# Spacing the final LayerNorm on VectorE and re-pacing the output products of a mixed RG-LRU and attention layer

## The chip, the cores and the metric

The kernel runs on one core of a Trainium2 chip. The metric is device time in microseconds (us) for one execution of the whole layer, and the median of several runs is what is compared. The engines are named as the profile names them: PE (TensorE, matrix products; PEld are its weight loads), DVE (VectorE), ACT (ScalarE), POOL (GpSimd) and SP (SyncE, which here issues nearly all DMAs).

## The reference

One layer on x of 2048 rows and 1024 columns, in float32:

```
h = layer_norm(x) * (1 + scale) + shift          # scale, shift, gate from c
xr, zr, q, k, v, za, fl = split(h @ w_in)
y_r = rms_norm(rg_lru(conv(xr))) * silu(zr)      # 512 columns, recurrent half
y_a = rms_norm(forgetting_attention(q, k, v, log_sigmoid(fl))) * silu(za)   # 8 heads of 64
y   = concat(y_r, y_a) @ w_out
res = alpha * x + gate * y
out = layer_norm(res) * ln_gain + ln_bias
```

The attention is causal, with a decay term added to each score, and a softmax over the keys.

## The kernel before, in words

Every float32 matrix is split into a float16 high and low part, and a product is three matmuls (high by high, high by low, low by high). The change lies in the last phase, from about 560 us on, where attention, the projections of q, the output products and the final LayerNorm are woven into one stream.

The queries are cut into 4 chunks of 512 rows (`ci` = 0 to 3), and the work of the attention is a list of 32 items, chunk by chunk and head by head. An item (ci, h) has `4*ci + 4` steps, one for each block of 128 keys. A step is `s_t`: two matmuls of 512 columns into a PSUM tile `pst` (L1335, L1337), the exponential on ACT into `pf` (L1343), a cast on ACT to float16 into `ph` (L1345), and the low part of `ph` on POOL (L1347) or, each fourth step, on DVE (L1349). Five steps later `av` multiplies that block with V into two `acc` tiles. `fin` copies the sums and divides them (L1365 to L1370).

Ahead of each item runs its `maxpass`: the scores once more, into PSUM tiles `pmx`, whose row maxima DVE takes with `tensor_reduce` into `mc` (L1315, 4*(ci+1) of them per item); from these come `Z`, a small transpose into `pzt`, and one row of `qb` (L1330), which the item's own score products then subtract. So a group of four `pzt` matmuls marks the end of each item's maxima, 32 groups in all. `pst`, `pmx` and `pzt` share five PSUM banks (tag A).

Everything else is a side job: a list `side` of Python generators, of which `pump` runs the first one from one `yield` to the next. In its order the list holds the projections of q for chunks 1 to 3 (`q_unit`, 24 matmuls into one PSUM bank, tag O, then an eviction by ACT and DVE), the preparation of the weights `w_out`, and last `out_gen`, the output products. `out_gen` goes through 16 tiles of 128 rows. A tile has two halves of 512 columns; a half is 24 matmuls (`out_mm`: 12 on `yr`, the recurrent part, 12 on `yT`, the attention part), with three yields inside, then one DVE instruction that scales the sum and adds the residual (`xres`, L1524) and a yield. So a tile is 8 yields and 48 matmuls. `prep_a` loads `zs` and the residual `xres` of the next tile, `prep_b` and `prep_c` make its `yT` (ACT, four transposes `pyt` on PE into bank O, DVE, ACT, POOL). The tiles of a chunk can start only after that chunk's last head (`out_open`).

After its second half, a tile's LayerNorm is queued as `ln_gen`: statistics, then four DVE instructions of 128 by 512 elements, two that subtract the mean and multiply by the gain (L1438), two that scale by the inverse deviation and add the bias (L1442), and the store of the tile (L1445, an SP queue entry that waits for them). `out_gen` takes one step of the oldest `ln_gen` at each of its own yields.

How often `pump` is called is set in the main loop: at each of the steps `credit` grows by `todo / togo`, and `pump` is called once for each whole unit. From item (0,0) on this is (12*QU+32)/64 with QU = 5, from item (1,4) on 102/256, to the end. What is left after the last step runs then in one go.

All of this only gives the order in which the program is written. A scheduler then orders the instructions of each engine by dependencies, priorities and its own estimates; the engines run their queues in that order.

Of the kernel before, what the change touches and what calls it, by code (L numbers as in the profile page):

```python
# [26 lines left out]
TT = S // P  # L27
# [11 lines left out]
def hybrid_mixer(  # L39
# [921 lines left out]
    def q_unit(p, ci):  # L961
        w, u = take(("q", p))
        if p not in q_sc:
            q_sc[p] = cst([P, 1], f"fq{p}")
            nc.vector.tensor_tensor(q_sc[p], u, k_sc[p], ALU.mult)
        ps = pj_bank() if ci == 0 else bank("O", "pq")
        for _ in proj_1(ps, w, ci):
            yield
        hl = t2([P, 2, CH], "qhl", F16)
        split_out(hl[:, 0], hl[:, 1], ps, q_sc[p])  # L970
        qk_store([(qd, 0, 1)], p, hl, slice(ci * CH, (ci + 1) * CH))
        yield

    w_out_v = w_out.rearrange("(k p) n -> k p n", p=P)
    wocol = cst([P, KT], "wocol")
# [310 lines left out]
    def maxpass(ci, h, res):  # L1286
        n = cnt[0]
        cnt[0] += 1
        qb, z = QB[n % 4], Z[n % 4]
        sl = slice(ci * CH, (ci + 1) * CH)  # L1290
        nk = (ci + 1) * CH
        if ci < 2:
            kk = r4([P, 2, 2 * CH], "kk", F16)
        else:
            kk = sb.tile([P, 2, S], F16, name="kk", tag="H", bufs=8)
        nc.sync.dma_start(kk[:, 0, 0:nk], kd[h, :, 0:nk])
        nc.sync.dma_start(kk[0:DH, 1, 0:nk], kd[h, 0:DH, 0:nk])
        nc.sync.dma_start(kk[DH:DH + 3, 1, 0:nk], kb[h, :, 0:nk])
        nc.sync.dma_start(qb[0:DH, :], qd[h, DH:P, sl])
        qs = sb.tile([P, CH], F16, name="qs", tag="qs", bufs=3)  # L1300
        nc.sync.dma_start(qs, qd[h, :, sl])
        nc.gpsimd.memset(qb[DH:DH + 1, :], 0.0)
        res.append((kk, qb, qs))
        yield
        mc = sm([P, 4, 4], "mc")
        for i in range(4):
            nk = (4 * ci + i + 1) * P
            for b in range(ci + 1):
                w = min(CH, nk - b * CH)
                ps = bank("A", "pmx")  # L1310
                end = b == ci
                mm(ps[:, 0:w], qb[:, i * P:(i + 1) * P], kk[0:67, 1, b * CH:b * CH + w], True, not end)
                if end:
                    mm(ps[:, w - P:w], identb, maskn, False, True)
                nc.vector.tensor_reduce(out=mc[:, i, b:b + 1], in_=ps[:, 0:w], axis=AX.X, op=ALU.max)  # L1315
                yield
        if ci > 0:
            m = sm([P, 4], "mrow")
            nc.vector.tensor_reduce(out=m, in_=mc[:, :, 0:ci + 1], axis=AX.X, op=ALU.max)
        else:  # L1320
            m = mc[:, :, 0]
        nc.vector.tensor_scalar(z[:, :, DH], m, -1.0 / RS, ndc[:, ci, h:h + 1], ALU.mult, ALU.add)
        yield True
        yield True
        with tc.issue_after(last["pe"]):
            ps = bank("A", "pzt")
            for i in range(4):
                mm(ps[0:DH + 1, i * P:(i + 1) * P], z[:, i, 0:DH + 1], ident16, i == 0, i == 3, True)
        yield
        nc.scalar.copy(qb[DH:DH + 1, :], ps[DH:DH + 1, :])  # L1330
# [96 lines left out]
    def ln_gen(tt, xt):  # L1427
        st = sm([P, 2, 6], "bst")
        nc.vector.bn_stats(st[:, 0, :], xt[:, 0:CH])
        yield  # L1430
        nc.vector.bn_stats(st[:, 1, :], xt[:, CH:D])
        mv = sm([P, 2], "mv")
        nc.vector.bn_aggr(mv, st)
        rs = ln_rs(mv)
        yield
        for n in range(2):
            ns = slice(n * CH, (n + 1) * CH)
            nc.vector.scalar_tensor_tensor(xt[:, ns], xt[:, ns], mv[:, 0:1], late["lng"][:, ns], ALU.subtract, ALU.mult)  # L1438
            yield
        for n in range(2):  # L1440
            ns = slice(n * CH, (n + 1) * CH)
            nc.vector.scalar_tensor_tensor(xt[:, ns], xt[:, ns], rs, late["lnb"][:, ns], ALU.mult, ALU.add)  # L1442
            if n == 0:
                yield
        nc.sync.dma_start(out[tt * P:(tt + 1) * P, :], xt)  # L1445
# [8 lines left out]
    def out_mm(pq, yr, yT, i, ns):  # L1454
        for k in range(KT):
            if k < 4:
                yy = yr[:, k, :, i * P:(i + 1) * P]
            else:
                yy = yT[:, :, (k - 4) * P:(k - 3) * P]
            mm(pq, yy[:, 0, :], wo[k][:, 0, ns], k == 0, False)  # L1460
            mm(pq, yy[:, 0, :], wo[k][:, 1, ns], False, False)
            mm(pq, yy[:, 1, :], wo[k][:, 0, ns], False, k == KT - 1)
            if k % 2 == 1 and k < KT - 1:
                yield k

    def out_last(tt, yr, yT, xt):
# [17 lines left out]
        for ns in hs:  # L1484
            nc.vector.scalar_tensor_tensor(xt[:, ns], xt[:, ns], rs, late["lnb"][:, ns], ALU.mult, ALU.add)
            nc.sync.dma_start(out[tt * P:(tt + 1) * P, ns], xt[:, ns])

    def out_gen():
        lns = []

        def step_ln():
            if lns and next(lns[0], 0) == 0:
                lns.pop(0)

        for tt in range(TT):
            ci, i = tt // 4, tt % 4
            while ci not in outs:
                starved[0] = True
                step_ln()
                yield  # L1500
            starved[0] = False
            if tt not in yTs:
                prep_b(tt)
                yield
                prep_c(tt)
                yield
            yr = outs[ci][0]
            yT, xt = yTs[tt]
            if tt == TT - 1:
                for _ in out_last(tt, yr, yT, xt):  # L1510
                    step_ln()
                    yield
                break
            for n in range(2):
                ns = slice(n * CH, (n + 1) * CH)
                pq = bank("C" if ci == NC - 1 else "O", "pout")
                for k in out_mm(pq, yr, yT, i, ns):
                    yield
                    if n == 0 and k == 1:
                        prep_a(tt + 1)  # L1520
                    elif n == 0 and k == 3:
                        prep_b(tt + 1)
                    step_ln()
                nc.vector.scalar_tensor_tensor(xt[:, ns], pq, kap, xt[:, ns], ALU.mult, ALU.add)  # L1524
                if n == 0:
                    g = ln_gen(tt, xt)
                    next(g)
                    yield
                    prep_c(tt + 1)
                else:  # L1530
                    next(g)
                    lns.append(g)
                    yield
        while lns:
            step_ln()

    items = [(ci, h) for ci in range(NC) for h in range(H)]
    LOOK = 5
    QU = 5
    Y = {}  # L1540
    res = []
    side = []
# [70 lines left out]
    for n, (ci, h) in enumerate(items):  # L1613
# [4 lines left out]
                todo, togo = 12 * QU + 32, 8 * 4 + 4 * 8  # L1618
        if (ci, h) == (1, 4):
            todo, togo = 3 * 34, 4 * 8 + 8 * 12 + 8 * 16  # L1620
        while done < cum[n]:
            next(mg)
            done += 1
# [51 lines left out]
```

## Time and profile before

| What | us |
|---|---|
| median of 3 runs | 1149.67 (1149.29 to 1150.42) |
| the profiled execution's own time | 1150.82 |
| its span in the trace | 1149.1 |
| PE busy over the span | 1091.7 |
| DVE, ACT, POOL busy | 787.0, 707.1, 627.7 |

The page gives the busy time of each engine and its share, then slices of the span, the groups of instructions and the chain of work that ended last. A group's time is by kernel line and by tile names, so `pout` are the output products, `pst` and `acc` the attention's, `pmx` those of the row maxima. The views by windows give the same for chosen stretches of the span; the `pzt` groups are used here to cut the span between items. The granted clock is the share of TensorE's full clock in the stretch.

### The profile page before, as it was taken

To read this page: it belongs to the slowest core of one execution; us is meant where nothing else is said; L and a number is where in the kernel's file an instruction comes from. 1 tells how busy PE (TensorE), PEld (TensorE's weight loads), DVE (VectorE), ACT (ScalarE), POOL (GpSimd) and SP (SyncE) were. 2 spreads that over 40 slices of the span, in tenths; PEclk is the share of its full clock that TensorE was granted. 3 is DMA by queue.
4 is the path that set the end of the run, shared out by engine and by line. 5 is a ranking of instruction groups with operands and counts; after the bars stand their busy time and mean duration, and the time that the engine had idled before them with its cause. 6 is when DMAs were issued, how large, how long until landed. Compare 5 with 4: busy or idle time off the path is not lost.

```text
span 1149.1 us, 20239 instructions
## 1 busy us (share of the span) xinstructions
PE 1091.7 (95%) x7473; PEld 611.2 (53%) x7473; DVE 787.0 (68%) x1441; ACT 707.1 (62%) x1234; POOL 627.7 (55%) x655
## 2 busy tenths in 40 slices
PE   8989999999999999999989999999999989999897
PEld 5875544454544444444455545556555555655544
DVE  6878577776777973585287556777777777787546
ACT  3447737664767511543286668787778877787930
POOL 5725633454455300730279756777777676766731
PEclk8999999999999999999979999999999999999999
DMA  9853047220224711764154354333233142321011
GB/s 285 242 172 110 1 127 217 77 68 19 55 56 119 229 66 52 251 203 142 36 187 145 108 161 136 97 96 100 91 106 114 35 137 82 103 74 47 19 47 55
DMA packets 109415, 128.36 MB, mean 112 GB/s; under 512 B 10316, under 2 KB 79540, under 8 KB 109316
## 3 DMA queue, kind: packets, MB, share of 16 engines
q1 hardware_dynamic: 109088, 127.01, 36.2%
q8 instruction: 58, 0.95, 0.3%
q14 instruction: 41, 0.34, 0.1%
q10 hardware_dynamic: 228, 0.06, 0.0%
HBM read 97.57 MB, written 29.46 MB: 111 GB/s over the span
## 4 chain that ended last, share of the span: by engine, by line
PE 65%; DVE 11%; ACT 8%; issue 6%; POOL 5%; DMA 4%; SPq 0%; DVEq 0%; ACTq 0%; POOLq 0%
PE pj L93 25%; PE pout L93 12%; PE pst L93 8%; PE pq L93 6%; PE acc L93 5%; PE pmx L93 4%; DVE mc L1315 2%; POOL ph L1347 1%; PE pgate L93 1%; ACT pf L1343 1%; DVE xres L1442 1%; DMA zs<-zd 1%; POOL XL L636 1%; ACT ph L1345 1%; DVE wadab L648 1%
## 5 line engine op out<-in xcount | busy, mean ns | idle before, releaser
L93 PE MATMUL pj<-hT,wT 128*128 128x512 f16 x1440 | 321.1, 381 | 2.6 <-DVE sza L1192 2.6
L1347 POOL TENSOR_TENSOR ph<-pf,ph 128x512 f16<-128x512 f32 (+2 forms) x240 | 263.8, 1111 | 108.5 <-ACT ph L1345 92.6
L93 PEld LDWEIGHTS <-wT 128*128 128x128 f16 x1792 | 169.8, 98 | 205.3 <-issue 18.8
L1315 DVE TENSOR_REDUCE mc<-pmx 128x1 f32<-128x512 f32 (+2 forms) x320 | 183.3, 601 | 90.2 <-PE pmx L93 84.1
L1343 ACT ACTIVATE pf<-pst,bias 128x512 f32<-128x512 f32 (+1 forms) x320 | 194.3, 632 | 59.4 <-PE pst L93 57.7
L1345 ACT CAST ph<-pf 128x512 f16<-128x512 f32 (+1 forms) x320 | 173.3, 568 | 21.4 <-PE acc L93 15.4
L93 PE MATMUL acc<-V,ph 128*128 128x129 f16 (+1 forms) x2176 | 159.6, 209 | 9.0 <-POOL ph L1347 4.4
L93 PEld LDWEIGHTS <-ph 128*128 128x128 f16 x2176 | 126.5, 99 | 67.8 <-POOL ph L1347 8.8
L93 PE MATMUL pst<-qs,kk 128*128 128x512 f16 (+1 forms) x320 | 111.6, 351 | 4.1 <-DVE mc L1315 2.9
L93 PE MATMUL pst<-qb,kk 65*128 65x512 f16 (+1 forms) x320 | 110.5, 354 | 0.9 <-ACT qb L1330 0.8
L93 PE MATMUL pmx<-kk,qb 67*128 67x512 f16 (+2 forms) x320 | 104.1, 353 | 4.5 <-DVE mc L1315 2.7
L93 PE MATMUL pout<-wo,yT 128*128 128x512 f16 (+1 forms) x396 | 97.2, 372 | 1.5 <-ACT yT L1423 1.5
L93 PE MATMUL pout<-wo,yr 128*128 128x512 f16 (+1 forms) x396 | 91.5, 373 | 1.5 <-DVE zs L1422 1.5
L93 PE MATMUL pj<-wN,hT 128*128 128x512 f16 x384 | 89.4, 378 | 0.2 <-ACT XL L847 0.2
L1243 POOL TENSOR_TENSOR XL<-XL,szr 128x512 f32<-128x512 f32 x16 | 22.8, 1428 | 111.7 <-ACT szr L1240 111.7
L93 PE MATMUL pq<-hT,wT 128*128 128x512 f16 x288 | 69.0, 393 | 3.1 <-DVE qhl L917 3.0
L1349 DVE TENSOR_TENSOR ph<-pf,ph 128x512 f16<-128x512 f32 (+1 forms) x80 | 54.8, 685 | 24.0 <-ACT ph L1345 23.2
L93 PEld LDWEIGHTS <-hT 128*128 128x128 f16 x640 | 44.6, 96 | 48.5 <-issue 3.3
L93 PEld LDWEIGHTS <-kk 65*128 65x128 f16 (+1 forms) x640 | 53.8, 99 | 29.2 <-issue 8.2
L93 PEld LDWEIGHTS <-yr 128*128 128x128 f16 x396 | 37.6, 98 | 39.3 <-issue 2.2
L93 PEld LDWEIGHTS <-yT 128*128 128x128 f16 x396 | 37.3, 97 | 38.6 <-ACT yT L1423 1.7
L491 POOL TENSOR_TENSOR xl<-xc,xh 128x512 fp32r<-128x512 f32 x16 | 23.1, 1446 | 57.0 <-ACT xh L489 55.6
(311 smaller groups left out, 1796.1 us busy)
## 6 DMA issues: line engine op xcount, KB each, us to landing
wraw<-in_w_in_dram SPq DMA_DIRECT2D x40, 512.0 KB
woraw<-in_w_out_dram SPq DMA_DIRECT2D x16, 512.0 KB
xres<-in_x_dram SPq DMA_DIRECT2D x16, 512.0 KB
out_dram<-xres SPq DMA_DIRECT2D x15, 512.0 KB
xt<-in_x_dram SPq DMA_DIRECT2D x16, 256.0 KB
wadab<-in_w_ada_dram SPq DMA_DIRECT2D x8, 512.0 KB
xt<-in_x_dram SPq DMA_DIRECT2D x8, 512.0 KB
wsh<-in_w_ada_dram SPq DMA_DIRECT2D x16, 256.0 KB
```

What stands on the lines that cost most here:

```text
L93: m = nc.tensor.matmul(o, lhsT=l, rhs=r, start=st, stop=sp, skip_group_check=chk)
L491: nc.gpsimd.tensor_tensor(out=xl, in0=xc, in1=xh, op=ALU.subtract)
L636: nc.gpsimd.tensor_scalar(XL[j][:, sl], XL[j][:, sl], 1.0, cs[j], ALU.mult, ALU.add)
L648: nc.vector.scalar_tensor_tensor(sub, blk[:, q - 1], cact[:, q - 1:q], sub, ALU.mult, ALU.add)
L1243: nc.gpsimd.tensor_tensor(out=XL[j][:, sl], in0=XL[j][:, sl], in1=sz, op=ALU.mult)
L1315: nc.vector.tensor_reduce(out=mc[:, i, b:b + 1], in_=ps[:, 0:w], axis=AX.X, op=ALU.max)
L1343: nc.scalar.activation(pf32[:, 0:w], ps[:, 0:w], AF.Exp, scale=DH ** -0.5, bias=bias[:, ci, h, kt:kt + 1])
L1345: nc.scalar.copy(ph[:, 0, 0:w], pf32[:, 0:w])
L1347: nc.gpsimd.tensor_tensor(out=ph[:, 1, 0:w], in0=pf32[:, 0:w], in1=ph[:, 0, 0:w], op=ALU.subtract)
L1349: nc.vector.tensor_tensor(ph[:, 1, 0:w], pf32[:, 0:w], ph[:, 0, 0:w], ALU.subtract)
L1442: nc.vector.scalar_tensor_tensor(xt[:, ns], xt[:, ns], rs, late["lnb"][:, ns], ALU.mult, ALU.add)
```

## The change

It has three parts.

First, each of the four LayerNorm instructions of a tile is traced under `issue_after(last["mc"])`, where `last["mc"]` is the row maximum that was traced last. This is an ordering on DVE's own queue, with no semaphore: the scheduler must place the piece behind that row maximum.

Second, `q_unit` for chunks 1 to 3 gets one more, empty yield at its end, and QU goes from 5 to 6, so that `todo` counts it.

Third, the pace of the output products. A counter `owed` starts at 128 (8 units for each of 16 tiles) and falls by one at each yield of a half and at each half's end. At the first head of chunk 2, `todo` is set to `owed - 64` over 96 steps; at the first head of chunk 3 to `owed - 32 - 9` over 112 steps; at the last head, (3,7), to 5 over 16 steps. Before, the pace of 102/256 held for all of these.

```diff
@@ q_unit
         qk_store([(qd, 0, 1)], p, hl, slice(ci * CH, (ci + 1) * CH))
         yield
+        if ci > 0:
+            yield
@@ maxpass
-                nc.vector.tensor_reduce(out=mc[:, i, b:b + 1], in_=ps[:, 0:w], axis=AX.X, op=ALU.max)
+                last["mc"] = nc.vector.tensor_reduce(out=mc[:, i, b:b + 1], in_=ps[:, 0:w], axis=AX.X, op=ALU.max).ins
@@ ln_gen
-            nc.vector.scalar_tensor_tensor(xt[:, ns], xt[:, ns], mv[:, 0:1], late["lng"][:, ns], ALU.subtract, ALU.mult)
+            with tc.issue_after(last["mc"]):
+                nc.vector.scalar_tensor_tensor(xt[:, ns], xt[:, ns], mv[:, 0:1], late["lng"][:, ns], ALU.subtract, ALU.mult)
             yield
...
-            nc.vector.scalar_tensor_tensor(xt[:, ns], xt[:, ns], rs, late["lnb"][:, ns], ALU.mult, ALU.add)
+            with tc.issue_after(last["mc"]):
+                nc.vector.scalar_tensor_tensor(xt[:, ns], xt[:, ns], rs, late["lnb"][:, ns], ALU.mult, ALU.add)
@@ out_gen
+    owed = [8 * TT]
...
                 for k in out_mm(pq, yr, yT, i, ns):
+                    owed[0] -= 1
                     yield
...
                 nc.vector.scalar_tensor_tensor(xt[:, ns], pq, kap, xt[:, ns], ALU.mult, ALU.add)
+                owed[0] -= 1
@@ main loop
-    QU = 5
+    QU = 6
...
         if (ci, h) == (1, 4):
             todo, togo = 3 * 34, 4 * 8 + 8 * 12 + 8 * 16
+        elif ci > 1 and h == 0:
+            todo, togo = owed[0] - 8 * (TT - 4 * ci) + (0 if ci == 2 else -9), 8 * steps - (0 if ci == 2 else 16)
+        elif (ci, h) == (3, 7):
+            todo, togo = 5, 16
```

What this does to the order is seen at two places. The first is DVE's queue in chunk 3, at a tile's LayerNorm. Before, it reads as follows (`mrow` and `Z` end an item's maxima, `mv` and `ve` are the tile's statistics):

```order
L1319 TENSOR_REDUCE mrow<-mc 128x4
L1433 BN_AGGR mv<-bst 128x2
L1322 TENSOR_SCALAR Z_1667<-mrow,ndc 128x4
L1449 TENSOR_SCALAR ve<-mv 128x1
L1438 SCALAR_TENSOR_TENSOR xres<-xres,mv,lng 128x512 x2
L1442 SCALAR_TENSOR_TENSOR xres<-xres,rs,lnb 128x512 x2
L1315 TENSOR_REDUCE mc<-pmx 128x1
```

All four pieces stand in one row there. Now DVE's queue in chunk 3 of the changed kernel, at the first two pieces of a tile (`rv` is the reciprocal of a head's end; the lines are six lower or less):

```order
L1317 TENSOR_REDUCE mc<-pmx 128x1
L1441 SCALAR_TENSOR_TENSOR xres<-xres,mv,lng 128x512
L1317 TENSOR_REDUCE mc<-pmx 128x1 x3
L1369 RECIPROCAL rv<-ytmp 128x2
L1317 TENSOR_REDUCE mc<-pmx 128x1 x4
L1441 SCALAR_TENSOR_TENSOR xres<-xres,mv,lng 128x512
L1317 TENSOR_REDUCE mc<-pmx 128x1 x2
```

Seven row maxima now stand between the two pieces. In the 12 tiles of chunks 0 to 2, the two pieces of a kind stood side by side 12 times (gain) and 8 times (bias) before, and now 4 and 2 times.

The second place is PE's queue in the last head, up to the first score product that needs the new `qb` row (`qb_1664`). Before:

```order
L93 LDWEIGHTS ph
L93 MATMUL acc<-V_4899,ph 128x65
L93 LDWEIGHTS ph
L93 MATMUL acc<-V_5389,ph 128x129
L93 LDWEIGHTS ph
L93 MATMUL acc<-V_5389,ph 128x129
L93 LDWEIGHTS kk
L93 MATMUL pst<-qb_1664,kk 128x512
```

After, the rows just ahead of the same product are the last of 20 output products (12 on `yr`, then 8 on `yT`):

```order
L93 LDWEIGHTS yT
L93 MATMUL pout<-wo,yT 128x512
L93 LDWEIGHTS yT
L93 MATMUL pout<-wo,yT 128x512
L93 LDWEIGHTS kk
L93 MATMUL pst<-qb_1664,kk 128x512
```

Counted between the `pzt` groups, PE's queue holds the same number of output products up to group 18 of 32 in both kernels (120). From group 18 to 25, the heads of chunk 2, it holds 192 before and 264 now; from group 25 to 32, the heads of chunk 3 up to the last, 264 before (48, 41, 31, 38, 34, 48 and 24 in the single stretches) and 120 now (0, 24, 39, 9, 24, 24 and 0); behind the last group 216 before and 288 now.

## The prediction

> **What bounds the kernel now.** I read the page first: one engine is busy nearly all the time.
>
> ```profile
> PE 1091.7 (95%) x7473; PEld 611.2 (53%) x7473; DVE 787.0 (68%) x1441; ACT 707.1 (62%) x1234; POOL 627.7 (55%) x655
> ```
>
> PE's work is the same before and after, so a gain can only come from time in which PE waits, and a loss from new waits. Next I cut the phase of the change into stages at `pzt` groups (the windows view) and counted the output products in each (the same view for `pout`). Columns: window, its length, busy time and instructions of PE, PEld, DVE, ACT, POOL, then the granted clock and the DMA share.
>
> ```profile
> 560.00:688.50 128.50, 120.58 (x903) 69.23 (x903) 80.72 (x170) 86.31 (x184) 91.48 (x112) 0.92 0.45 137
> 770.70:899.30 128.60, 125.20 (x1144) 75.66 (x1142) 96.26 (x184) 101.25 (x198) 95.04 (x108) 1.00 0.36 107
> 899.30:1073.00 173.70, 167.89 (x1498) 99.87 (x1498) 129.73 (x229) 136.88 (x261) 120.63 (x128) 0.99 0.24 75
> 1073.00:1096.50 23.50, 18.18 (x194) 11.58 (x195) 9.83 (x13) 20.29 (x43) 19.91 (x21) 0.86 0.09 32
> 1096.50:1104.30 7.80, 6.26 (x32) 2.78 (x30) 1.31 (x4) 4.38 (x12) 2.36 (x6) 0.97 0.26 76
> 1104.30:1143.00 38.70, 37.76 (x204) 20.06 (x204) 23.37 (x40) 3.62 (x6) 7.50 (x7) 1.00 0.10 41
> ```
> ```profile
> 770.70:899.30 128.60, 47.14 (x192) 5.97 (x8) 1.00 0.36 107
> 899.30:1073.00 173.70, 64.43 (x264) 8.21 (x11) 0.99 0.24 75
> 1073.00:1096.50 23.50, 0.02 (x1) 0.00 (x0) 0.86 0.09 32
> ```
>
> The first row is the stage of the q projections, PE busy 94%. The second row is seven heads of chunk 2, the third seven heads of chunk 3: PE busy 97%, no other engine above 79%. Then comes the last head (1073.0 to 1096.5). It has neither row maxima nor output products left; PE is busy for 18.2 of 23.5 us, at a granted clock of 0.86, and ACT for 20.3. Then 7.8 us, in which chunk 3's sums become its first `yT`, and 38.7 us of output products back to back.
>
> Who makes PE wait is in the waits view (total, times, longest), from 560 us on:
>
> ```profile
> PE acc L93 <- POOL ph L1347: 4.4, 8, 1.3
> PE acc L93 <- DVE ph L1349: 4.1, 3, 1.4
> PE pq L93 <- DVE qhl L917: 3.0, 3, 2.1
> PE pst L93 <- DVE mc L1315: 2.9, 5, 1.3
> PE pmx L93 <- DVE mc L1315: 2.7, 3, 1.4
> PE pout L93 <- DVE zs L1422: 1.5, 3, 0.7
> ```
>
> So the row maxima on DVE cost PE 2.9 + 2.7 = 5.6 us, and the eviction of a q projection 3.0 us. The chain shows why the maxima come late (start, length, what):
>
> ```profile
> 729.96 0.98 POOL rs L1451
> 730.96 3.20 DVE xres L1442 x2
> 734.17 0.61 DVE mc L1315
> ```
>
> Two LayerNorm pieces in a row hold a row maximum for 3.2 us.
>
> A product's price is read where they run back to back, in the chain's
>
> ```profile
> 1110.48 15.54 PE pout L93 x72
> ```
>
> which is 15.54/72 = 0.216 us each.
>
> **The change, part by part.** The sum is made against the profiled execution's 1150.8 us; the median of the runs, 1149.67, is 1.15 lower, and I subtract the same from the end.
>
> *Chunk 2 gets 72 products more* (264 for 192). PE is the bound there with 97% and has next to no gap to take them: 72 x 0.216 = **+15.6**.
>
> *Chunk 3 loses 144 products* (120 for 264): 144 x 0.216 = 31.1 us of PE work. That is the gain only as long as PE stays the bound. Without products a head of chunk 3 is (173.7 - 264 x 0.216)/7 = 16.7 us of PE's time, its small losses included. Two of the seven stretches have none now and one has 9 (18.6 us); those with 24 need 21.9 and the one with 39 needs 25.1. What else can a head not go below? ACT, with 16 exponentials and 16 casts. The last head shows ACT alone, in time order:
>
> ```profile
> 1074.10 0.58 ACT L1330 CAST qb<-pzt 1x512 f16<-1x512 f32 x1
> ...
> 1076.67 2.42 ACT L1343 ACTIVATE pf<-pst,bias 128x512 f32<-128x512 f32 x4 [0.69 <-PE pst L93]
> ...
> 1091.14 0.48 ACT L1343 ACTIVATE pf<-pst,bias 128x128 f32<-128x128 f32 x1
> 1091.40 1.96 ACT L1345 CAST ph<-pf 128x512 f16<-128x512 f32 x4
> ```
>
> From 1076.67 to 1093.36 it is 16.7 us, and with `qb` 17.3: the lowest floor. The highest is the whole last head, 23.5. Between them lies ACT's busy time per head in chunk 3, 136.88/7 = 19.6, from the stage itself, with row maxima in between; I take that, as the row nearest to the heads in question. The two empty heads then lose 2 x (19.6 - 16.7) = 5.8 and the one with 9 loses 1.0: -31.1 + 6.8 = **-24.3**. At 17.3 it is -29.9, at 23.5 (where all but the 39 are lifted) -7.8.
>
> *Behind the last `pzt`, 72 more.* 48 go into the last head, 24 follow its sums. The first 20 stand ahead of the first product with the new `qb` row; with four transposes, eight `acc` and three more score products before it that is about 6.2 us after `pzt` where it was 3.3 (1076.25 against 1072.96):
>
> ```profile
> 1072.96 0.41 PE L93 MATMUL pzt<-ident,Z 128*65 128x128 f16 x4 [0.32 <-DVE ve L1449]
> ...
> 1075.89 0.52 PE L93 MATMUL acc<-V,ph 128*128 128x65 f16 x8 [1.35 <-DVE ph L1349]
> 1076.25 0.81 PE L93 MATMUL pst<-qb,kk 65*128 65x512 f16 x3
> ```
>
> That is +2.9 on the head's start; I call it +3.2, with one cast and one scaling on ACT that come along. The other 28 (6.0 us) go into PE's 5.3 idle us and the slow stretch. In the 7.8 us behind, PE had 24 products (5.2 us); with 48 and four transposes it has 10.8, so the wait for `yT` is covered and +3.0 remains. Together **+6.2**. Bounds: +3 if the first 20 also hide, +16 if nothing does.
>
> *LayerNorm pieces behind row maxima.* No work is added, and the pieces' own time stays. What is queued behind a piece that moves back is the store of its tile, and behind that on SP's queue the next loads. SP stands at that store for long already (total, times, longest):
>
> ```profile
> SPq L1445 <- DVE xres L1442: 136.9, 11, 24.1
> ```
>
> PE paid 1.5 us for a late `zs`, the load that comes behind it. So at best the 5.6 us of the row maxima go, at worst the store moves back and PE waits for twice as much more, +3. Pieces pass a row maximum one at a time now, but pairs are left: I take **-2**.
>
> *A yield more after a q projection.* In the first row's stage it lets steps in between an eviction and the next 24 matmuls into the same bank: at best the 3.0 us of `qhl` go; later projections can push the first output products back as much, +3, though their pace per step rises with QU (104/64 for 92/64). I take **-1**.
>
> Sum: 15.6 - 24.3 + 6.2 - 2 - 1 = **-5.5**: 1150.8 - 5.5 = 1145.3 for the profiled execution, 1144.2 for the median.
>
> The clock in the last head: 0.86 over 23.5 us is 3.3 us of lost clock, though PE's longest single wait there is the 1.35 us quoted above. The Trainium skill, "TensorE: Matmul & The Clock Gate", Part 1, has the clock fall to half only after an idle window of about 3.4 us; the trace differs, since it falls with no such gap. By that page, filled gaps keep the full clock, and the sum would be -5.5 - 3.3 = -8.8, 1140.9. The sum itself holds none of it: only 10 of the 48 products lie late in that head, where PE waits for POOL's `ph` (the first row of the waits).
>
> **The rivals.**
>
> *ScalarE becomes the bound in chunk 3 (slower).* With the products gone, a head takes what ACT and the chain behind it take. With a floor f between 18.6 and 21.9 us, 2 x (f - 16.7) + (f - 18.6) is lost; the other parts sum to +18.8, so the change loses from f = 21.4 on. At 23.5 the sum is -7.8 + 18.8 = +11.0: 1160.7. For it: the last head had PE idle and still took 23.5 us. Against: 17.3 of ACT in that head, and the head's stretch just before it, with all its row maxima and 24 products, began at
>
> ```profile
> 1052.78 0.39 PE L93 MATMUL pzt<-ident,Z 128*65 128x128 f16 x4
> ```
>
> and so took 1072.96 - 1052.78 = 20.2 us. Chance 0.10.
>
> *The last head does not take its 48 products (slower).* PE's queue is in order: a product that stands ahead of a score product holds up ACT, and ACT is that head's bound. With +16 for +6.2 the sum is +4.3: 1154.0. For it: the 20 products ahead of `qb`'s first use. Against: PE's idle time there. Chance 0.06.
>
> *One PSUM bank (slower).* All products of chunks 0 to 2 go through bank O, which is free again only when DVE has done
>
> ```profile
> L1524 DVE SCALAR_TENSOR_TENSOR xres<-pout,kap,xres 128x512 f32<-128x512 f32 x19 | 14.2, 746 | 10.5 <-PE pout L93 10.4
> ```
>
> At 3.1 products a step for 2.3 the halves come closer in chunk 2: 264/24 = 11 halves, and if PE met each eviction in full, 11 x 0.746 = +8.2, sum +2.7: 1152.4. Against: PE never waited for this line before, and in the new order other matmuls stand behind each half's end. The Trainium skill, "Perfetto Trace Analysis", Optimizing Tensor Performance, says that independent matmul groups should rotate through different banks so that an eviction overlaps the next group's matmuls; it speaks against this change, and the trace so far shows no such wait at one bank. Chance 0.05.
>
> *It cancels (no change).* The products removed from chunk 3 buy less (f near 21, or the LayerNorm term at +1) and pay for chunk 2 and the end alone: within 2.3 us, 1149.7. The pieces would then be spaced without effect, because PE had other work. Chance 0.15.
>
> *All goes well (faster).* f = 17.3: the sum is -29.9 + 18.8 = -11.1, 1138.6; with all of the 5.6 and 3.0 us gone too, -16.7, 1133.0. For it: ACT's 17.3. Against: in-order queues leave small waits in every head so far (16.7 of PE's time holds them). Chance 0.15; for the forecast itself 0.49.
>
> **How the numbers follow.** About 0.2%, 2.3 us, is what a measurement of this kernel can tell from no change. Faster: 0.49 + 0.15 = 0.64; the same 0.15; slower 0.10 + 0.06 + 0.05 = 0.21. The forecast is 1144.2. The range goes from 1137, a little under the case f = 17.3, to 1154, which holds two of the slower rivals; outside are most of the first rival and half of the best case. Without the slower and the equal cases the forecast's own range is 1137 to 1147.
>
> **What would show it.** In the profile after, cut at the same `pzt` groups: chunk 2's seven heads at 144 us for 128.6; chunk 3's at about 149 for 173.7, with the empty heads at 19 to 20 us; from the last `pzt` to the first `yT` product of chunk 3 about 37.5 for 31.3; PE's waits for `mc` under 4 us. The forecast is wrong if the empty heads take 21.4 us or more with ACT near 100%, if chunk 2 grows by clearly more than 16 us with PE waiting for line 1531's eviction, or if the last head goes beyond 30 us. If LayerNorm were the true cause of a gain, chunk 3's length minus 0.216 us per product would fall, and with it the waits for `mc`, more than the 2 us taken here.

## The result, and the profile after

The changed kernel takes 1156.55 us (median of 4 runs, 1154.38 to 1161.06), the kernel before 1149.58 beside it. The ratio is 1.0064, with a 95% interval of 1.0045 to 1.0084. So it is 7 us slower, where 1144.2 was forecast. The profiled execution of the changed kernel took 1161.06 us, the slowest of its four; its span is 1159.3, which is 10.2 more than before.

The page's row of the engines shows PE busy a little longer for the same number of instructions:

```profile
PE 1096.5 (95%) x7473; PEld 614.1 (53%) x7473; DVE 782.8 (68%) x1441; ACT 707.3 (61%) x1234; POOL 628.1 (54%) x655
```

Cut at the same `pzt` groups (columns as in the prediction: window, length, busy time and instructions of PE, PEld, DVE, ACT, POOL, granted clock, DMA share), the four stages from the first group to the end are:

```profile
567.10:775.10 208.00, 194.52 (x1560) 113.93 (x1559) 131.13 (x276) 151.87 (x316) 142.39 (x180) 0.95 0.40 122
775.10:924.50 149.40, 143.47 (x1242) 84.95 (x1240) 105.58 (x200) 107.05 (x204) 98.54 (x112) 0.99 0.33 101
924.50:1072.80 148.30, 138.25 (x1345) 83.79 (x1342) 114.35 (x198) 131.71 (x258) 116.48 (x124) 1.00 0.24 67
1072.80:1159.30 86.50, 75.87 (x501) 41.61 (x501) 46.02 (x78) 28.08 (x58) 32.53 (x34) 0.95 0.19 66
```

The first row is the q projections and chunk 1, 208.0 us for 204.8 before. The second is chunk 2, 149.4 for 128.6: +20.8. The third is chunk 3, 148.3 for 173.7: -25.4. The last, behind the last `pzt`, is 86.5 for 76.1: +10.4. Chunk 2 and chunk 3 carry 72 products more and 144 fewer, and chunk 3 paid what was forecast. So the loss is not there: chunk 2 took 5.2 more than the forecast's +15.6, the end 4.2 more than its +6.2, and the first stage 3.2 where nothing was forecast but a gain.

The waits from 560 us on (total, times, longest) show what PE waits for:

```profile
PE acc L93 <- POOL ph L1349: 8.2, 15, 1.2
PE pzt L93 <- DVE Z L1324: 5.4, 4, 2.6
PE acc L93 <- DVE ph L1351: 5.1, 6, 1.9
PE pout L93 <- DVE zs L1424: 3.7, 4, 1.9
PE pst L93 <- DVE mc L1317: 3.6, 7, 0.7
PE pmx L93 <- DVE mc L1317: 1.3, 3, 0.9
```

The row maxima `mc` fell from 5.6 to 3.6 + 1.3 = 4.9 us. But `acc` now waits 13.3 us for `ph` where it waited 8.5, `pout` 3.7 us for `zs` where it was 1.5, and `pzt` 5.4 us for `Z` where it was 0.3. `ph` of each fourth step, `zs`, `Z` and the LayerNorm pieces all stand in DVE's one queue. The larger part of the wait for `ph`, 8.2 us for 4.4, is for POOL's `ph`, which does not; by what path it grows, these lists do not show.

The clearest single case is the last `pzt`. This is DVE's timeline ahead of it (start, length, what):

```profile
1066.96 0.68 DVE L1317 TENSOR_REDUCE mc<-pmx 128x1 f32<-128x512 f32 x1
1067.56 1.04 DVE L1441 SCALAR_TENSOR_TENSOR xres<-xres,mv,lng 128x512 f32<-128x512 f32 x1
1068.52 1.64 DVE L1446 SCALAR_TENSOR_TENSOR xres<-xres,rs,lnb 128x512 f32<-128x512 f32 x1
1070.08 0.16 DVE L1321 TENSOR_REDUCE mrow<-mc 128x4 f32<-128x16 f32 x1
1070.16 0.68 DVE L1431 BATCH_NORM_STATS2 bst<-xres 128x6 f32<-128x512 f32 x1
1070.76 0.96 DVE L1446 SCALAR_TENSOR_TENSOR xres<-xres,rs,lnb 128x512 f32<-128x512 f32 x1
1071.64 1.12 DVE L1324 TENSOR_SCALAR Z<-mrow,ndc 128x4 f16<-128x4 f32 x1
```

The item's last row maximum is done at 1067.64. `Z`, which needs nothing else but the short `mrow`, starts 4.0 us later, because three LayerNorm pieces and a statistics instruction stand between them. PE's timeline at that place:

```profile
1072.82 0.64 PE L93 MATMUL pzt<-ident,Z 128*65 128x128 f16 x4 [2.63 <-DVE Z L1324]
...
1073.57 0.63 PE L93 MATMUL pst<-qs,kk 128*128 128x512 f16 x1
...
1080.56 0.38 PE L93 MATMUL pst<-qb,kk 65*128 65x512 f16 x1
```

PE stood for 2.63 us, and a score product behind it shows as 0.63 us where one of the same width, 7 us later, shows as 0.38: PE runs slower for a while (the granted clock of that stretch is 0.50, in a row of the last section).

That this is not one accident is seen in the order. Counted over the 18 items from the end of chunk 1 on, DVE's queue holds 1 LayerNorm piece between an item's last row maximum and its `Z` before, and 17 after. The ordering says "not ahead of that maximum"; a piece that is placed right behind it stands ahead of `Z` whenever the last traced maximum is an item's last.

### The profile page after: what moved, and what is told of

Its sections match the earlier page's. It is cut to its first block, busy times and chain, and to the rows that moved or that the text cites. A ratio compares the mean times of both kernels' runs of the same rounds, so it can differ in the third digit from the quotient of the medians.

```text
span 1159.3 us, 20220 instructions
## 1 busy us (share of the span) xinstructions
PE 1096.5 (95%) x7473; PEld 614.1 (53%) x7473; DVE 782.8 (68%) x1441; ACT 707.3 (61%) x1234; POOL 628.1 (54%) x655
## 4 chain that ended last, share of the span: by engine, by line
PE 68%; DVE 11%; ACT 8%; DMA 4%; issue 4%; POOL 4%; SPq 0%; ACTq 0%; DVEq 0%; POOLq 0%
PE pj L93 28%; PE pout L93 13%; PE pst L93 8%; PE acc L93 6%; PE pmx L93 4%; PE pq L93 3%; DVE mc L1317 2%; PE pgate L93 1%; ACT pf L1345 1%; POOL ph L1349 1%; POOL woraw L1051 1%; DMA woraw<-in_w_out_dram 1%; DVE wadab L648 1%; DVE xres L1446 1%; ACT L515 1%
## 5 line engine op out<-in xcount | busy, mean ns | idle before, releaser
L93 PE MATMUL acc<-V,ph 128*128 128x65 f16 (+1 forms) x2176 | 161.0, 208 | 15.5 <-POOL ph L1349 8.2
L93 PE MATMUL pj<-h,w 128*128 128x512 f32 x192 | 52.3, 421 | 0.9 <-ACT h L388 0.8
```

What stands on the lines that cost most here:

```text
L93: m = nc.tensor.matmul(o, lhsT=l, rhs=r, start=st, stop=sp, skip_group_check=chk)
```

## The experiments

The theories: P, the new pace costs more than forecast (the end, or ACT as the bound); L, the LayerNorm pieces stand in front of urgent work on DVE; Q, at first that the extra yield costs, later that there are two separate places; and later D, ordering the pieces costs wherever they stand. Every kernel is compared with the kernel before on the same chip; ratios are to that, with their 95% intervals. The cuts of code for `e1_ln` to `e3_pace` are against the kernel before, the others against the changed kernel, and they leave out lines.

### One part at a time

`e1_ln` has only the LayerNorm ordering:

```diff
+ with tc.issue_after(last["mc"]):   # both kinds of piece; no extra yield, QU = 5, old pace
```

> The LayerNorm ordering alone, pace and q projections as before. Theory P (the new pace of the output products costs the time: chunk 2 and the end grow by more than chunk 3 gives back, +5.7 us in the two traces) expects no change, within 2 us of before. Theory L (a piece queued behind the last row maximum of an item stands ahead of that item's Z, so PE waits at pzt: 5.4 us in the changed kernel for 0.3 before) expects +3 to +6 us and a wait of PE for Z at pzt of 3 us or more in its trace.

Measured: 1157.3 us, ratio 1.0059 (1.0036 to 1.0083), and 3.3 us of waiting for `Z`: a little more than L expected. `e2_q` has only the second part:

```diff
+        if ci > 0:
+            yield
-    QU = 5
+    QU = 6
```

> The extra yield per q unit with QU 6 alone. P and L both expect no change, within 2 us of before. Theory Q (this part costs the 4.5 us by which the changed kernel's trace is later at the start of chunk 2) expects +3 us or more, and the start of chunk 2, at the pzt group 18, at 773 us or later for 770.7.

Measured: 1145.63, ratio 0.9964 (0.995 to 0.9979). No theory expected this gain, and Q in its first form falls. `e3_pace` has only the counter `owed` and the paces that use it:

```diff
+    owed = [8 * TT]
...
+        elif ci > 1 and h == 0:
+            todo, togo = owed[0] - 8 * (TT - 4 * ci) + (0 if ci == 2 else -9), 8 * steps - (0 if ci == 2 else 16)
+        elif (ci, h) == (3, 7):
+            todo, togo = 5, 16
```

> The new pace alone, without the LayerNorm ordering and the extra yield. P expects +5 to +7 us, with chunk 2 about 20 us longer, chunk 3 about 25 shorter, the end about 10 longer. L and Q expect it at -2 to +2 us, since what costs is not in it.

Measured: 1149.57, ratio 1.0004 (0.9984 to 1.0023). `e4_noln` is the changed kernel without the ordering:

```diff
-            with tc.issue_after(last["mc"]):
-                nc.vector.scalar_tensor_tensor(xt[:, ns], xt[:, ns], mv[:, 0:1], late["lng"][:, ns], ALU.subtract, ALU.mult)
+            nc.vector.scalar_tensor_tensor(xt[:, ns], xt[:, ns], mv[:, 0:1], late["lng"][:, ns], ALU.subtract, ALU.mult)
```

> The changed kernel without the LayerNorm ordering: pace and extra yield stay. P expects +5 to +7 us, as the changed kernel. L expects 3 to 6 us less than the changed kernel, so +1 to +4 us against before, and a wait of PE for Z at pzt under 1 us.

Measured: 1144.76, ratio 0.9961 (0.9946 to 0.9976), further down than L expected. P falls: the pace is worth nothing either way, the yield and QU gain 4, and the ordering alone loses 7. With the other parts in place it costs (1.0064 - 0.9961) x 1150 = 12 us.

What one such delay does is seen in the chain of waits of `e1_ln` in chunk 2 (start, length, what):

```profile
893.03 3.19 DVE mc L1315 x6
896.22 1.47 DVE xres L1439
897.68 1.20 DVE mc L1315 x2
...
901.08 1.39 DVE xres L1444
...
903.15 0.60 DVE zs L1422
903.79 6.93 PE pout L93 x19
```

DVE is the chain here for 10 us, two pieces of 1.47 and 1.39 us lie on it, and behind it 19 products take 6.93 us where 19 x 0.216 is 4.1. Three rows of this stretch give the reason:

```profile
898.99:902.40 3.41, 1.89 (x25) 1.42 (x26) 3.41 (x5) 1.64 (x5) 2.95 (x3) 1.00 0.00 0
902.40:903.80 1.40, 0.01 (x1) 0.01 (x1) 1.40 (x5) 0.19 (x1) 0.96 (x2) 0.50 0.04 12
903.80:909.23 5.43, 5.43 (x13) 1.86 (x13) 0.08 (x1) 0.00 (x0) 0.00 (x0) 0.50 0.00 0
```

PE is busy for 1.89 of the first 3.41 us, and from 902.40 to 909.23 the granted clock is 0.50. So the delays of this place cost twice: the waits, and the slower clock behind them.

Over the whole phase it is mostly the waits. The sum of the four stages (first the length, then the busy time of PE) in the changed kernel:

```profile
sum 592.20, PE 552.11 PEld 324.28 DVE 397.08 ACT 418.71 POOL 389.95; mean PE 138.03 PEld 81.07 DVE 99.27 ACT 104.68 POOL 97.49
```

and in `e4_noln`:

```profile
sum 579.60, PE 548.31 PEld 324.27 DVE 396.86 ACT 417.94 POOL 394.99; mean PE 137.08 PEld 81.07 DVE 99.21 ACT 104.48 POOL 98.75
```

The phase is 12.6 us longer, and of that 8.8 is PE idle (40.1 for 31.3), and for 552.11 - 548.31 = 3.8 PE shows as busy longer with the same products. This is not lost clock: what the granted clock takes away in the phase is the same in both, 16.0 and 15.6 us. DVE's own busy time is the same to 0.2 us. It is the place of the pieces that costs, not their work.

### Where the pieces stand

`e5_behind_z` queues the pieces behind the last traced `Z` instead, so that none stands between a last maximum and its `Z`:

```diff
-                last["mc"] = nc.vector.tensor_reduce(out=mc[:, i, b:b + 1], ...).ins
+                nc.vector.tensor_reduce(out=mc[:, i, b:b + 1], ...)
-        nc.vector.tensor_scalar(z[:, :, DH], m, -1.0 / RS, ndc[:, ci, h:h + 1], ALU.mult, ALU.add)
+        last["mc"] = nc.vector.tensor_scalar(z[:, :, DH], m, -1.0 / RS, ndc[:, ci, h:h + 1], ALU.mult, ALU.add).ins
```

> The changed kernel with one edit: the LayerNorm pieces are queued behind the Z of the item whose maxima were traced last, and no longer behind the last row maximum. In DVE's order no piece then stands between an item's last row maximum and its Z, where the changed kernel has 17 from chunk 1's end on and before has 1. Theory L (the piece ahead of Z costs the time) expects the loss gone: 1144 to 1147 us, as without the ordering (1144.8). Theory D (any LayerNorm ordering takes DVE from other late work, zs and ph, and Z is only one of them) expects half of the loss or more to stay: 1150 us or more.

Measured: 1150.99, ratio 1.0015 (0.9997 to 1.0034). `e6_gain` orders only the two gain pieces of a tile, and `e7_bias` only the two bias pieces. The edit of `e6_gain`, and then that of `e7_bias`:

```diff
-            with tc.issue_after(last["mc"]):
-                nc.vector.scalar_tensor_tensor(xt[:, ns], xt[:, ns], rs, late["lnb"][:, ns], ALU.mult, ALU.add)
+            nc.vector.scalar_tensor_tensor(xt[:, ns], xt[:, ns], rs, late["lnb"][:, ns], ALU.mult, ALU.add)
```

```diff
-            with tc.issue_after(last["mc"]):
-                nc.vector.scalar_tensor_tensor(xt[:, ns], xt[:, ns], mv[:, 0:1], late["lng"][:, ns], ALU.subtract, ALU.mult)
+            nc.vector.scalar_tensor_tensor(xt[:, ns], xt[:, ns], mv[:, 0:1], late["lng"][:, ns], ALU.subtract, ALU.mult)
```

> The changed kernel with only the two gain pieces of a tile queued behind row maxima; the two bias pieces are free. 18 pieces stand between a last row maximum and Z, as many as with all four ordered. L expects nearly the whole loss, 1153 to 1157 us. D expects about half of it, 1149 to 1152.

> The changed kernel with only the two bias pieces queued behind row maxima. 9 pieces stand between a last row maximum and Z. L expects half of the loss, 1149 to 1152 us, less than with the gain pieces alone. D expects the same as for the gain pieces alone, within 1 us.

Measured: `e6_gain` 1161.59, ratio 1.0101 (1.008 to 1.0122); `e7_bias` 1153.96, ratio 1.0023 (1.001 to 1.0037). `e6_gain` lies above what both theories expected, and so does `e7_bias` above L; D's "the same within 1 us" falls by these two. Pieces between a last maximum and `Z`: 0 in `e5_behind_z`, 9 in `e7_bias`, 17 in the changed kernel, 18 in `e6_gain`; the ratios rise in that order: 1.0015, 1.0023, 1.0064, 1.0101. That speaks for L. But with none of them in front of `Z` about half of the loss is still there (1.0015 against 0.9961), so `Z` is not all of it; where that half lies is seen further down, under "Which tiles".

`e10_hold` prices a late `Z` by itself: no ordering, and one reduction of no use in front of 17 of the `Z`:

```diff
+        if n >= 15:
+            with tc.issue_after(lm):        # lm: the item's last row maximum
+                hold = nc.vector.tensor_reduce(out=sm([P, 1], "hold"), in_=late["lng"], axis=AX.X, op=ALU.max).ins
+            with tc.issue_after(hold):
+                nc.vector.tensor_scalar(z[:, :, DH], m, -1.0 / RS, ndc[:, ci, h:h + 1], ALU.mult, ALU.add)
```

> The changed kernel without the LayerNorm ordering, and with one extra reduction of 128 x 1024 on VectorE (about 1.1 us by the 0.61 us of 128 x 512; its result is not used) between the last row maximum and Z of the 17 items from the second half of chunk 1 on. It prices a late Z alone. Theory L with Z as the whole cause: the 17 pieces of 1.47 us cost 11.8 us in the changed kernel, so 17 holds of 1.1 us cost 11.8 x 1.1/1.47 = 8.8, 1153.6, with PE's waits for Z at 4 us or more. L with Z as half of it, the rest being casts and zs behind piled-up pieces: about +4.4, 1149.2. Theory D: a late Z is hidden by the look-ahead of the maxima, 1144 to 1146.

Measured: 1156.05, ratio 1.0076 (1.0055 to 1.0098): 13 us over `e4_noln`. The group of these instructions:

```profile
L1326 DVE TENSOR_REDUCE hold<-lng 128x1 f32<-128x1024 f32 x17 | 20.5, 1207 | 0.0
```

17 delays of 1.21 us, 20.5 us in all, cost more than the 8.8 of the expectation. In the trace, though, the kernel is 2.6 us later than `e4_noln` already at the seventh head of chunk 1, where the first of them stands (174.0 us from the first `pzt` group for 171.4); from there to the end it loses 9.6. Among the waits:

```profile
PE acc L93 <- POOL ph L1355: 9.3, 16, 1.2
...
PE pzt L93 <- DVE Z L1328: 2.1, 4, 0.7
```

Those put down to the held `Z` stay small. More of the delay shows up further on: `acc` waits 9.3 us for POOL's `ph` where it was 4.9 in `e4_noln`, and PE's busy time is 556.80 for 548.31. Here most of these 8.5 us are slower clock: the granted clock takes away 21.7 us for 15.6.

```profile
sum 591.80, PE 556.80 PEld 327.16 DVE 412.67 ACT 419.06 POOL 393.77; mean PE 139.20 PEld 81.79 DVE 103.17 ACT 104.77 POOL 98.44
```

So a late `Z` alone is dear, and the rival that the look-ahead of the maxima hides it falls.

`e9_early` takes the maximum for the ordering only from the first half of an item, so that pieces are spaced and none comes late:

```diff
-                last["mc"] = nc.vector.tensor_reduce(out=mc[:, i, b:b + 1], ...).ins
+                r = nc.vector.tensor_reduce(out=mc[:, i, b:b + 1], ...).ins
+                if i < 2:
+                    last["mc"] = r
```

> The changed kernel, but the row maximum that a LayerNorm piece is ordered behind is taken only from the first half of an item's maxima (rows blocks 0 and 1 of 4). The pieces stay ordered behind a maximum (15 gaps between pieces as wide as in the changed kernel), but none of them stands between an item's last maximum and its Z any more (0 of 18 items; 17 pieces in the changed kernel). Theory L (the loss comes from pieces pushed to the late end of an item's maxima, where Z and the next head's casts follow on the same queue): the loss goes, 1144 to 1147, as the kernel without any ordering (1144.8), waits for Z under 2 us and for zs under 3 us. Theory D (ordering the pieces one by one costs by itself, wherever the maximum is): 1150 to 1157.

Measured: 1152.5, ratio 1.0042 (1.0024 to 1.0059). L as the whole cause falls with this: no piece stands in front of a `Z`, and 9 us over `e4_noln` remain. The waits have changed places instead:

```profile
PE acc L93 <- POOL ph L1351: 7.0, 15, 1.2
PE pst L93 <- DVE mc L1317: 5.7, 10, 1.1
...
PE pmx L93 <- DVE mc L1317: 2.1, 4, 0.9
PE pzt L93 <- DVE Z L1326: 1.7, 3, 1.0
```

`Z` is down to 1.7 us, but the maxima are at 5.7 + 2.1 = 7.8, more than before the change. `e4_noln` has 6.2 us there, and only 4.9 for POOL's `ph`:

```profile
PE acc L93 <- POOL ph L1349: 4.9, 10, 1.2
...
PE pmx L93 <- DVE mc L1317: 4.2, 5, 1.3
...
PE pst L93 <- DVE mc L1317: 2.0, 5, 0.7
PE pzt L93 <- DVE Z L1324: 1.6, 2, 1.0
```

### Which tiles

Laid beside each other, the traces differ first in the last two heads of chunk 1 (`pzt` groups 16 to 18). In `e4_noln`:

```profile
736.80:751.00 14.20, 14.15 (x131) 8.76 (x128) 10.73 (x21) 11.76 (x25) 11.40 (x16) 1.00 0.21 62
751.00:767.50 16.50, 16.50 (x155) 9.95 (x153) 15.06 (x29) 14.35 (x33) 12.96 (x15) 1.00 0.40 125
```

In the changed kernel:

```profile
739.90:759.30 19.40, 19.40 (x180) 11.84 (x178) 13.98 (x27) 13.34 (x30) 13.39 (x16) 1.00 0.29 92
759.30:775.10 15.80, 13.21 (x112) 8.05 (x111) 13.47 (x25) 13.52 (x29) 8.79 (x11) 0.91 0.20 64
```

Together 35.2 us for 30.7. PE's queue holds 22 and 26 output products there in `e4_noln`, and 40 and 8 now. The seventh head takes them all; the eighth has too few to fill PE, which is idle for 2.6 us, at a granted clock of 0.91. The ordering acts on DVE, but the scheduler re-arranged PE's queue too. Before the change the counts were 15 and 33, and the two heads took 33.75 us (13.31 and 20.44), with 1.46 us of PE idle in the second.

`e12_first4` keeps the ordering only for the four tiles that are normalised there, `e13_early_rest` takes it from these four alone and keeps the early one of `e9_early` for the rest:

```diff
-            with tc.issue_after(last["mc"]):
+            with tc.issue_after(last["mc"]) if tt < 4 else contextlib.nullcontext():    # e13: tt >= 4
```

> The changed kernel with the ordering kept only for the LayerNorm pieces of the first four tiles (chunk 0's, done while chunk 1 ends and chunk 2 begins); the other tiles' pieces are free. The order of PE's queue at the end of chunk 1 is that of the changed kernel (40 output products in the seventh head, 8 in the eighth; without ordering 22 and 26), and 9 of the 17 pieces before a Z remain, 7 of them by the second head of chunk 2. Theory Q (two places: the order of products at chunk 1's end costs 4.4 us, late Z in chunk 2 about 0.6 us a piece): 4.4 + some 3 above the kernel without ordering, 1151 to 1153 (ratio 1.001 to 1.003); the last two heads of chunk 1 at 35 us instead of 30.8. Theory L alone (only late Z counts, 9 of 17 pieces): +6, also 1151, but with 31 us for those two heads and the loss in chunk 2.

> The kernel with pieces ordered behind maxima of the first half of an item (1152.5), but with the first four tiles' pieces free. PE's queue at chunk 1's end is that of the kernel without ordering (22 and 26 products), no piece stands before a Z, and the later tiles' pieces are ordered as before. Theory Q: the 4.1 us at chunk 1's end go, those two heads take 31 us, and the time is 1147 to 1149 (ratio 0.997 to 1.000). Theory D (ordering costs wherever it stands): 1151 to 1153.

Measured: `e12_first4` 1149.75, ratio 1.0003 (0.999 to 1.0017), 5 us over `e4_noln`, a little under what both theories expected. `e13_early_rest` 1153.49, ratio 1.0028 (1.0012 to 1.0045), 8 us over `e4_noln`: Q's 1147 to 1149 is missed. One of its twelve executions took 5076.55 us; the ratio is of the other eleven.

The table has the traces of all kernels with the new pace and the yield, in us, cut at the `pzt` groups: the last two heads of chunk 1 (groups 16 to 18), chunk 2 (18 to 25), in it the two heads from group 21 to 23, and what lies behind the last group. In brackets are the output products of the two heads.

| kernel | end of chunk 1 | chunk 2 | of it, 21 to 23 | behind the last |
|---|---|---|---|---|
| `e4_noln` | 30.7 (22, 26) | 143.9 | 39.8 (27, 48) | 83.6 |
| changed | 35.2 (40, 8) | 149.4 | 45.2 (49, 28) | 86.5 |
| `e6_gain` | 35.1 (43, 5) | 152.4 | 46.3 (47, 27) | 87.0 |
| `e7_bias` | 35.8 (45, 3) | 146.0 | 42.0 (45, 27) | 84.7 |
| `e12_first4` | 35.2 (40, 8) | 145.7 | 41.1 (29, 48) | 83.7 |
| `e5_behind_z` | 34.6 (37, 11) | 144.0 | 37.7 (27, 42) | 86.3 |
| `e9_early` | 34.8 (39, 9) | 144.4 | 40.8 (28, 48) | 85.9 |
| `e13_early_rest` | 30.7 (22, 26) | 149.2 | 45.4 (47, 28) | 85.9 |
| `e10_hold` | 31.0 (24, 24) | 148.8 | 39.4 (24, 48) | 85.3 |

So Q is half right. Chunk 1's end is a place of its own: some 4 to 5 us come with the ordering of the first four tiles and go without it, whatever the other tiles do. Here lie also 4 us of what `e5_behind_z` and `e9_early` still lose, and another 2 to 3 behind the last `pzt`; their chunk 2 is as long as without the ordering, to 0.5 us. So D, by which ordering costs wherever it stands, does not hold either.

In chunk 2 itself, `e13_early_rest` has no piece in front of a `Z` and still loses 5.3 us. They lie in the two heads from group 21 to 23:

```profile
827.70:854.00 26.30, 24.44 (x188) 13.48 (x187) 16.58 (x30) 15.55 (x30) 15.88 (x19) 0.94 0.30 89
854.00:873.10 19.10, 18.08 (x164) 10.75 (x162) 14.46 (x28) 14.52 (x27) 10.32 (x13) 1.00 0.25 67
```

The changed kernel loses its 5.5 us of chunk 2 in the same two heads:

```profile
838.50:862.90 24.40, 22.54 (x193) 13.13 (x190) 15.91 (x30) 16.69 (x33) 15.27 (x18) 1.00 0.39 117
862.90:883.70 20.80, 19.18 (x182) 11.59 (x181) 15.24 (x29) 14.64 (x28) 12.33 (x15) 1.00 0.31 86
```

and `e4_noln` has

```profile
830.30:847.80 17.50, 17.50 (x163) 10.77 (x162) 16.26 (x30) 13.77 (x27) 12.96 (x16) 1.00 0.42 134
847.80:870.10 22.30, 21.76 (x185) 12.46 (x182) 16.92 (x30) 14.61 (x29) 14.29 (x16) 1.00 0.30 91
```

In the four kernels that lose most there, PE's queue has some 47 products in the first of the two heads and 27 in the second, where the others have it the other way round. That is a rival to the late `Z` in chunk 2, of the kind seen at chunk 1's end: the products have moved on PE. No run moved the products alone, so how the loss of chunk 2 parts between the two is not shown.

### The pace

`e8_pace3` has no ordering, the extra yield, chunk 2 at the old pace, and only chunk 3 slowed, with 35 products held back for the end; `e11_hold60` holds 78 back:

```diff
-        elif ci > 1 and h == 0:
-            todo, togo = owed[0] - 8 * (TT - 4 * ci) + (0 if ci == 2 else -9), 8 * steps - (0 if ci == 2 else 16)
+        elif (ci, h) == (3, 0):
+            todo, togo = owed[0] - 8 * (TT - 4 * ci) - 9, 8 * steps - 16      # e11: - 17
```

> No LayerNorm ordering, the extra yield, and only the later half of the new pace: chunk 2 keeps the old pace, chunk 3 slows down so that 35 products more than before are left behind the last pzt group (251 for 216). It tests why the pace brought nothing: chunk 3 gave back 0.16 us for each of the 144 products taken from it, where chunk 2 paid 0.216 for each. If the first products taken from chunk 3 are worth the full 0.216 and only the later ones less, this kernel gains 7.6 us in chunk 3 and pays 3 to 4 at the end: 1141 to 1143 us, below the extra yield alone (1145.6). If the end costs as much as it gains, 1145 to 1147.

> No LayerNorm ordering, the extra yield, chunk 2 at the old pace, chunk 3 slowed further: 167 products in chunk 3's seven heads (210 in the fastest kernel so far, 1143.7), 294 behind (251). If the last head still takes products for nothing: 1143 or less. If it is full: 43 products x 0.216 = 9.3 us move behind the heads, while the two heads left without products stay at about 19.6 us instead of 16.7, which loses 5.8: 1149.5. I expect the second.

Measured: `e8_pace3` 1143.72, ratio 0.9935 (0.9913 to 0.9956), the fastest kernel here, between the two ranges of its expectation; it beats the kernel before and the changed one. Against `e2_q` and `e4_noln` the intervals just overlap. `e11_hold60` 1144.37, ratio 0.9959 (0.9942 to 0.9976), where I expected 1149.5. The two heads' floor that I used there was too high: an empty head of that kernel took 17.3 us (966.41 to 983.68), another 19.0. Between 35 and 78 products held back the time hardly moves, as it hardly moved between `e2_q` and `e4_noln`: the time is flat over a wide range of the pace, which fits that PE does the same products sooner or later.

## Why the prediction was wrong, point by point

The first three terms of the sum held in the kernels without the ordering.

- Chunk 2, +15.6: `e3_pace` and `e4_noln` have chunk 2 at 145.0 and 143.9 us, +16.4 and +15.3. The changed kernel's +20.8 holds another 5 us that come with the ordering.
- Chunk 3, -24.3: -25.4 in the changed kernel, -23.1 and -23.7 in the other two. The empty heads took 19.0 and 21.0 us where 19.6 was taken; ScalarE was no bound (131.71 of 148.3 us).
- Behind the last `pzt`, +6.2: +8.8 and +7.5 in `e3_pace` and `e4_noln`, a little under-sized, and +10.4 in the changed kernel. That the late `Z` of its last item makes the difference is not shown: `e5_behind_z`, `e9_early` and `e13_early_rest` have no such piece and took 85.9 to 86.3 us, for its 86.5.
- The bank rival: in the changed kernel PE waited for no eviction of an output product; of all traces only `e11_hold60` has such a wait, one of 0.9 us.

The yield after a q projection was mis-sized: -1 taken, -4.3 measured by `e2_q`. The 3.0 us of `qhl` went (0.2 left in the changed kernel), but I did not see that it also re-arranges the products at chunk 1's end from 15 and 33 to 22 and 26, where `e2_q` has 30.8 us (14.2 and 16.6) for 33.7.

The step that failed is "LayerNorm pieces behind row maxima", -2 with bounds of -5.6 and +3. Measured: +7 alone, +12 on top of the rest. The step counted what a piece holds up when it stands in front of a row maximum, and what its store holds up on SP. It did not ask what stands behind the piece in DVE's own queue at its new place: `Z`, `ph`, `zs`, each of which PE waits for. It even misread one of them: it took PE's 1.5 us for `zs` as a wait for a load behind the store, but the row names L1422, DVE's own multiplication for `yT`, and in the kernel before DVE never stands idle for a DMA ahead of it. In the changed kernel SP stands at the store for less time than before (115.1 us for 136.9), while PE's wait for `zs` went from 1.5 to 3.7. "At best the 5.6 us of the row maxima go" was also too kind: of the 5.6 only 0.7 went. The order was at hand: seven maxima had been counted between two pieces, and not what came after the second. Nor did the step see that with an edge on DVE the scheduler also moves output products on PE, which is 4.5 of the 12 us at chunk 1's end. None of the rivals was this mechanism: the slower ones had the new pace as their reason, and P fell.

What stays open: which of the late instructions, or of the moved products, costs how much in the twelve later tiles. Late `Z` alone is dear (`e10_hold`), and taking every piece away from `Z` gains only 2.5 to 6 us of 12 (`e9_early`, `e5_behind_z`), with intervals of about 2 us on each; but these two still have the products of chunk 1's end moved, which is 4 us of what they lose. Behind the last `pzt` 2 to 3 us come with the ordering and have no cause here. And the profile does not show why the free order, in which two pieces often stand side by side, is so cheap; that the scheduler puts them where DVE has time is an argument, not a measurement.

The spans of single executions hold some scatter too: from the first `pzt` group to the thirteenth, `e8_pace3` and `e11_hold60`, whose PE order is the same there, took 122.8 and 125.7 us. The 3 us that the changed kernel lost in that stage against before (125.5 for 122.6) are partly such scatter. But the three kernels without the extra yield took 121.8 to 122.6 us there and the twelve with it 122.8 to 125.7, 2.3 more on average: the yield seems to cost something in this stage, and `e2_q` gains in spite of it.

## What to carry to other kernels

An ordering edge says what an instruction must not precede, not what it will then stand in front of; before adding one, list what follows at the new place on the same in-order queue and who waits for it, and count it over the whole program (17 pieces in front of `Z` for 1 was there to be counted). When a change has several parts, time each alone first: here a gain of 4, a nothing and a loss of 7 lay under one number, and leaving one part out turned +7 into -5. An edge on one engine can re-arrange another engine's queue, so the order of the engine that is the bound is read again after every edit.

## What the runs showed of the hardware

The granted clock halves without any wait near 3.4 us. In the changed kernel it falls at 588.01, 680.17, 772.33 and 1072.70 us; these lie 27, 27 and 88 times 3.413 us apart, and in every trace here the falls lie on such a grid. What goes with a fall is how busy PE was in the 3.41 us before it. Here are two falls of the changed kernel, each with the stretch before it and what follows:

```profile
768.92:772.33 3.41, 1.88 (x17) 1.01 (x15) 3.41 (x5) 3.41 (x9) 1.54 (x2) 1.00 0.07 21
772.33:779.16 6.83, 5.76 (x51) 4.88 (x52) 5.74 (x10) 6.78 (x16) 6.07 (x6) 0.50 0.11 32
1069.29:1072.70 3.41, 0.52 (x8) 0.35 (x8) 3.41 (x5) 1.84 (x4) 3.37 (x3) 1.00 0.04 17
1072.70:1076.11 3.41, 3.29 (x20) 2.52 (x21) 1.08 (x3) 1.83 (x5) 1.46 (x3) 0.50 0.56 181
```

PE was busy for 55% of the first stretch and for 15% of the second. In `e1_ln` it was 1.89 of 3.41 us before the fall at 902.40, in waits of less than 0.8 us each; its wait of 1.44 us began only at the fall. The same does not always do it. Two stretches of the kernel before, of which only the second ends in a fall (at 929.70):

```profile
922.87:926.29 3.42, 1.93 (x26) 1.33 (x25) 3.42 (x5) 2.29 (x5) 2.38 (x2) 1.00 0.18 74
926.29:929.70 3.41, 1.77 (x21) 1.12 (x20) 2.35 (x5) 1.69 (x4) 2.21 (x4) 1.00 0.50 177
```

Over all 15 traces, from 560 us on to the last products, the clock falls 68 times. PE was busy for 15 to 66% of the stretch before. Of the stretches at full clock, all 19 in which it was busy for under 46% ended in a fall and none in which it was busy for over 67%; what decides between is not settled.

The Trainium skill, "TensorE: Matmul & The Clock Gate", Part 1, has the clock fall after at least one idle window of about 3.4 us, with windows that run freely. The grid of 3.413 us agrees with such windows; that the window must be idle does not go with PE busy for 55% of it, and the measurement decides. For a kernel that is bound by PE it means that several short waits close together can cost more than themselves: at half the clock, up to 1.7 us for each 3.41 us that it lasts.
